# A hybrid attention and gating trunk: projections merged into the attention's stream by whole accumulations

## The chip, the core and the metric

The kernel runs on one core of a Trainium2 chip. The metric is the time of one execution on the device, in microseconds (us). A core has TensorE (PE in the rows; its weight loads are PEld), VectorE (DVE), ScalarE (ACT), GpSimd (POOL) and SyncE (SP), which here only issues transfers. Each engine works through its own list of instructions in order; engines wait for one another by semaphores.

## What is computed

Two layers with RMS norms and residuals, on 1024 tokens of width 1024, in float32. The first mixes tokens by causal attention of 16 heads (128 + 64 wide queries and keys, 128 wide values), from low-rank latents `c_q` (384) and `c_kv` (256); the second by a gated unit with a triangular 128 x 128 matrix per group. Cut to what matters:

```
h = xn @ w_in
c_q, c_kv, k_r, gate = jnp.split(h, ...)
q  = (rms_norm(c_q) @ w_uq)            # per head: 128 without, 64 with rotation
kv = (rms_norm(c_kv) @ w_ukv)          # per head: key 128, value 128
s  = (q_nope @ k_nope + q_rope @ k_rope) * ATTN_SCALE
p  = softmax(where(causal, s, neg))
o  = (p @ v) * silu(gate)
x  = x + o @ w_o
x  = x + sgu_branch(rms_norm(x)) ; y = rms_norm(x)
```

## The kernel before

Every product is made of three matmuls: an operand is split into a rounded high half and a rest (`split`, L99 to L101: ACT copies the high half, DVE or POOL subtracts it), and `mm3` (L119 to L123) adds high times high, high times rest and rest times high in one PSUM bank.

Heads are worked through in pairs, n = 0 to 15, in `attention`. A head has ten steps. In a step PE transposes blocks of the probabilities (`transpose`, tile `pt`, one bank), ACT and DVE split them into `th` and `tl`, and one step later PE multiplies them with the values (`product`, tile `pv`). Between these stand the scores of the same head's later query tiles (4 to 7) and of the next head's first ones (0 to 3): `score(n, i)` writes a score tile `s` (two banks), adds the mask on DVE (L596), takes the maximum (L598), scales it (L599), and lets ACT take the exponential with its sum (L601); DVE inverts the sum and scales the probabilities `p0` to `p7` (L602, L603). The score of tile i is up to 1024 wide; from tile 4 on it has two parts of three products each, and two matmuls for the rotated half behind each (L588, L589).

What fills the stream is the projection work: keys (`key`) and queries (`query`) of the next head by `proj_items` (L427), values of a later pair by `val` (L513), and the output projection of the pair before by `out_proj` (L529), whose block of 512 columns is added to the residual `xt` by DVE (L543). These accumulate in the two banks of the pool `ps_g` (tiles `pj`, `pv`, `po`). Each returns a list of items (cost, function): before, a projection gives one item of cost 650 for each of its nk products, a value tile four items of 330, an output projection sixteen items of 650.

What sets the order: `merge` (L440) takes two lists and puts an item of the second behind the first item of the first list at which the second's share of cost, up to the item's middle, is no greater than the first's. For each step the main items (transposes, products, scores) are merged with as many filling items as the table `target` (L695) asks for. `cut` (L681) counts how many of the output projection's items stand ahead of the key and query of the second half. Then a scheduler orders instructions by readiness, so a list is not quite the order of the engines.

The last output projection (second half of the last pair) is returned as `self.rest` and merged in `sgu` (L939) with the normalization of the first half: `share_first` spreads the inverse norms by PE (tile `rb`, L187), `quarter` normalizes (L912) and splits (L101) the operands `x1`, `x2` of the first products (`pb`, `py`, `px`, L811). `x3` is another such operand.

Of the kernel before, what the change touches and what calls it, by code (L numbers as in the profile page):

```python
# [23 lines left out]
KT = D // P  # L24
# [42 lines left out]
class Builder:  # L67
# [359 lines left out]
    def proj_items(self, w, xs, nk, h, ps, evac):  # L427
        st = {}
        c = slice(h * HALF, (h + 1) * HALF)

        def go(k):
            if k == 0:
                st["b"] = ps.tile([P, HALF], F32, tag="g", name=self.nm("pj"))
            wh, wl = w()
            self.mm3(st["b"], wh[:, k], wl[:, k], xs[0][:, k, c], xs[1][:, k, c], k == 0, k == nk - 1)
            if k == nk - 1:
                evac(st["b"])
        return [(650, lambda k=k: go(k)) for k in range(nk)]

    @staticmethod  # L440
    def merge(a, b):
# [11 lines left out]
    def attention(self, st, cq, ckv, ka, kb):  # L453
# [24 lines left out]
        def load_val(p):  # L478
            WV[p] = self.weights(a["w_kv"][p], [P, 2, 256])

        def load_out(p):
            WO[p] = [self.weights(a["w_o"][2 * p + j], [P, D]) for j in range(2)]
# [30 lines left out]
        def val(p, t2):  # L513
            st = {}

            def go(i, k):
                if (i, k) == (0, 0):
                    st["b"] = ps.tile([P, HALF], F32, tag="g", name=self.nm("pv"))
                tok = slice((2 * t2 + i) * P, (2 * t2 + i + 1) * P)
                self.mm3(  # L520
                    st["b"][:, i * 256:(i + 1) * 256], ckv[0][:, k, tok], ckv[1][:, k, tok],
                    WV[p][0][:, k], WV[p][1][:, k], k == 0, k == 1,
                )
                if (i, k) == (1, 1):
                    V[p, t2] = tile_("vh", bufs=6), tile_("vl", bufs=6)
                    self.split(*V[p, t2], st["b"])
            return [(330, lambda i=i, k=k: go(i, k)) for i in range(2) for k in range(2)]

        def out_proj(p, h):  # L529

            st = {}

            def go(m, j):
                if j == 0:
                    pool, tag = self.banks[m % len(self.banks)]
                    st[m] = pool.tile([P, HALF], F32, tag=tag, name=self.nm("po"))
                oh, ol = O[p, j, h]
                wh, wl = WO[p][j]
                c = slice(m * P, (m + 1) * P)
                self.mm3(st[m], wh[:, c], wl[:, c], oh, ol, j == 0, j == 1)  # L540
                if j == 1:
                    x = self.x[m][:, half(h)]
                    nc.vector.tensor_tensor(x, x, st[m], op=ALU.add)  # L543
                    if p == NPAIR - 1 and h == 0:
                        square(m)
                    elif p == NPAIR - 1:
                        self.residual(m)
            return [(650, lambda m=m, j=j: go(m, j)) for m in range(KT) for j in range(2)]

        def first_sums():  # L550
            b = ps.tile([P, HALF], F32, tag="g", name=self.nm("ssq"))[:, :4]
# [121 lines left out]
        for n in range(NH):  # L673
            p, j = n // 2, n % 2
            nxt = n + 1 if n + 1 < NH else None
            sc = sum((score(n, i) for i in range(4, NT)), [])
            slots = [sc[:8], sc[8:12], sc[12:13], sc[13:], []]
            sn = [score(nxt, i) for i in range(4)] if nxt is not None else [[]] * 4
            slots += [[], sn[0] + sn[1], sn[2] + sn[3], [], []]
            fill = []  # L680
            cut = 8 + j  # L681
            if j == 0:
                fill += val(p, 2) + val(p, 3) if p else []
                wo = out_proj(p - 1, 1) if p else []
            else:
                wo = [(0, lambda: load_out(p))] + out_proj(p, 0)
            if nxt is not None:
                fill += [(0, lambda: load_head(nxt))] + key(nxt, 0) + query(nxt, 0) if n else []
                if j == 1:
                    fill += [(0, lambda: load_val(p + 1))] + val(p + 1, 0) + val(p + 1, 1)  # L690
                fill += wo[:cut] + key(nxt, 1) + query(nxt, 1) + wo[cut:]
            else:
                fill += wo
            steps = apply(n)
            target = [800, 1600, 1550, 1500, 2500, 2800, 2400, 1600, 2000, 1350]  # L695
            if nxt is None:
                target[:5] = [0] * 5
            scale = sum(c for c, _ in fill) / sum(target)
            used = cum = fi = 0
            tail = []  # L700
            if nxt is None:
                fill, tail = fill[:-8], fill[-8:]
            for s in range(10):
                main = [steps[s][0]] + pending + slots[s]
                pending = [steps[s][1]]
                cum += target[s] * scale
                f0 = fi
                while fi < len(fill) and (used < cum or s == 9):
                    used += fill[fi][0]
                    fi += 1  # L710
                emit(self.merge(main, fill[f0:fi]))
# [629 lines left out]
```

## Time and profile before

| | us |
|---|---|
| median of three runs | 1711.21 |
| lowest, highest | 1710.19, 1712.98 |
| the profiled execution | 1713.96 |
| its span in the profile | 1712.2 |
| TensorE busy | 1664.5 (97%) |
| VectorE busy | 1083.9 (63%) |
| ScalarE busy | 724.5 (42%) |
| GpSimd busy | 566.9 (33%) |

The span is the time from the first to the last instruction of the profiled execution; the execution's own time has 1.76 us more around it. Stages are read by windows of the span: up to about 321 us the first projections and gates; from about 321 to 984 the attention; then the second mixer. A window row gives each engine's busy time in it with the number of its instructions, and the clock that TensorE was granted (1.00 is 2.4 GHz). An engine busy in all of a window waits for nothing there.

### The profile page before, as it was taken

What the parts mean: (1) busy time and instruction counts of PE and PEld (TensorE: products, weight loads), DVE (VectorE), ACT (ScalarE), POOL (GpSimd) and SP (SyncE); (2) the same over time, 40 slices, a digit from 0 to 9 for tenths busy, and PEclk for the clock granted to TensorE, in tenths of its full rate; (3) what the DMA queues carried; (4) which work ended last, traced back from release to release, by engine and by line L of the source; (5) the groups of instructions that cost most, each with busy time, mean ns of one, the idle gap of its engine ahead of it and who ended that gap; (6) DMA issues with size and microseconds to landing.
All of it is one profiled execution on the core that took longest, in us unless ns stands there. A gap on an engine that the chain in (4) does not pass through costs nothing. (4 is left out here: it accounts for less than half of the span.)

```text
span 1712.2 us, 23934 instructions
## 1 busy us (share of the span) xinstructions
PE 1664.5 (97%) x9142; PEld 1442.3 (84%) x9142; DVE 1083.9 (63%) x1983; ACT 724.5 (42%) x1285; POOL 566.9 (33%) x423
## 2 busy tenths in 40 slices
PE   8899999999999999999999988999999999899997
PEld 7788888888888888888888867889999888688886
DVE  7352111687777777777777699545555444688967
ACT  6222221554545454444444456433333335544234
POOL 4435561211212121212121323232112242676663
PEclk9899999999999999999999999999999999999998
DMA  6234552211101011101010333223332144633202
GB/s 191 59 94 142 166 171 88 80 41 31 53 32 53 32 53 32 53 32 53 32 57 20 107 116 112 75 91 111 107 110 99 50 160 141 209 111 148 105 25 99
DMA packets 69539, 151.55 MB, mean 89 GB/s; under 512 B 11440, under 2 KB 21168, under 8 KB 68400
## 3 DMA queue, kind: packets, MB, share of 16 engines
q1 hardware_dynamic: 59808, 126.95, 22.9%
q10 hardware_dynamic: 9616, 23.07, 3.7%
q8 instruction: 72, 1.18, 0.3%
q14 instruction: 43, 0.35, 0.1%
HBM read 107.12 MB, written 38.15 MB: 85 GB/s over the span
## 5 line engine op out<-in xcount | busy, mean ns | idle before, releaser
L101 POOL TENSOR_TENSOR wl<-wf,wh 128x512 fp32r<-128x512 f32 (+1 forms) x156 | 194.4, 1264 | 404.9 <-ACT wh L100 404.7
L101 POOL TENSOR_TENSOR wl<-raw,wh 128x1024 fp32r<-128x1024 f32 x36 | 87.5, 2431 | 244.0 <-ACT wh L100 213.5
L601 ACT ACTIVATE p<-s,mx 128x128 f32<-128x128 f32 (+7 forms) x128 | 95.0, 742 | 124.5 <-DVE mx L599 122.7
L100 ACT ACTIVATE th<-pt 128x512 fp32r<-128x512 f32 (+1 forms) x160 | 88.4, 552 | 139.2 <-PE pt L625 138.5
L100 ACT ACTIVATE wh<-wf 128x512 fp32r<-128x512 f32 (+2 forms) x158 | 86.9, 581 | 101.5 <-PE pj L122 70.2
L121 PE MATMUL pj<-xnh,wh 128*128 128x512 f32 x304 | 120.5, 396 | 0.0
L811 PE MATMUL px<-x,wh 128*128 128x512 f32 x384 | 118.8, 391 | 1.6 <-ACT x L100 1.5
L122 PE MATMUL pj<-xnl,wh 128*128 128x512 f32 x304 | 120.1, 395 | 0.0
L123 PE MATMUL pj<-xnh,wl 128*128 128x512 f32 x304 | 119.9, 395 | 0.0
L101 DVE TENSOR_TENSOR tl<-pt,th 128x512 fp32r<-128x512 f32 (+1 forms) x160 | 101.1, 632 | 27.4 <-ACT th L100 26.4
L121 PE MATMUL po<-x,wh 128*128 128x512 f32 (+1 forms) x288 | 110.8, 385 | 0.0
L122 PE MATMUL po<-x,wh 128*128 128x512 f32 (+1 forms) x288 | 106.7, 370 | 1.4 <-POOL x L101 1.4
L543 DVE TENSOR_TENSOR xt<-xt,po 128x512 f32<-128x512 f32 x128 | 87.5, 683 | 32.3 <-PE po L123 31.5
L123 PE MATMUL po<-x,wl 128*128 128x512 f32 (+1 forms) x288 | 106.9, 371 | 0.0
L121 PE MATMUL po<-oh,wh 128*128 128x512 f32 x256 | 106.0, 414 | 0.0
L123 PE MATMUL po<-oh,wl 128*128 128x512 f32 x256 | 100.8, 394 | 0.0
L122 PE MATMUL po<-ol,wh 128*128 128x512 f32 x256 | 100.6, 393 | 0.0
L598 DVE TENSOR_REDUCE mx<-s 128x1 f32<-128x128 f32 (+7 forms) x128 | 96.9, 757 | 2.9
L1122 DVE TENSOR_TENSOR xt<-xt,po 128x512 f32<-128x512 f32 (+1 forms) x144 | 86.4, 621 | 16.7 <-PE po L123 15.1
L625 PE MATMUL pt<-ident,p 128*128 128x128 f32 x576 | 90.3, 273 | 0.5 <-DVE p L603 0.4
L811 PE MATMUL py<-x,wh 128*128 128x512 f32 x256 | 82.6, 402 | 6.3 <-DVE x L101 5.0
L811 PEld LDWEIGHTS px<-x,wh 128*128 128x128 f32 x384 | 71.8, 188 | 17.1 <-ACT x L100 1.9
(268 smaller groups left out, 4799.6 us busy)
## 6 DMA issues: line engine op xcount, KB each, us to landing
raw<-w_u_dram SPq DMA_DIRECT2D x18, 512.0 KB, 3.5
raw<-w_sg_dram SPq DMA_DIRECT2D x18, 512.0 KB, 3.6
wf<-w_gate_dram SPq DMA_DIRECT2D x32, 256.0 KB, 4.2
gate<-gate ACTq DMA_DIRECT2D x16, 512.0 KB, 3.7
wf<-w_o_dram SPq DMA_DIRECT2D x32, 256.0 KB, 2.8
gate<-gate SPq DMA_DIRECT2D x32, 256.0 KB, 2.7
raw<-w_v_dram SPq DMA_DIRECT2D x16, 512.0 KB, 3.4
v<-xt ACTq DMA_DIRECT2D x32, 256.0 KB, 2.0
```

Of the source, the lines that this page charges most:

```text
L100: self.nc.scalar.activation(hi, src, AF.Copy)
L101: (eng or self.nc.vector).tensor_tensor(lo, src, hi.bitcast(F32), op=ALU.subtract)
L121: nc.tensor.matmul(out, lh, rh, start=first, stop=False)
L122: nc.tensor.matmul(out, lh, rl, start=False, stop=False)
L123: nc.tensor.matmul(out, ll, rh, start=False, stop=last)
L543: nc.vector.tensor_tensor(x, x, st[m], op=ALU.add)
L598: nc.vector.tensor_reduce(mx, b, axis=AX.X, op=ALU.max)
L601: nc.scalar.activation(pr, b, AF.Exp, bias=mx, scale=SCALE, accum_out=sm)
L625: nc.tensor.transpose(b[:, w:w + P], PR[n, 4 * h + i][:, k * P:(k + 1) * P], self.ident)
L811: nc.tensor.matmul(o, l_, m_, start=opens and n == k == e == 0, stop=closes and n == 2 and k == 3 and e == (kind == "v"), skip_group_check ...
L1122: nc.vector.tensor_tensor(x, x, b, op=ALU.add)
```

## The change

Filling items become whole accumulations: a key or query projection is one item of cost 650 x nk, a value tile one of 1320, an output block (two heads) one of 1300. The numbers that count items are halved to match: `cut` is 4 + j, and the last head keeps four items back in place of eight. Since each function still issues the same instructions in the same order within an item, what changes is where the items stand.

```
--- before.py
+++ after.py
@@ -435,7 +435,7 @@
             self.mm3(st["b"], wh[:, k], wl[:, k], xs[0][:, k, c], xs[1][:, k, c], k == 0, k == nk - 1)
             if k == nk - 1:
                 evac(st["b"])
-        return [(650, lambda k=k: go(k)) for k in range(nk)]
+        return [(650 * nk, lambda: [go(k) for k in range(nk)])]
 
     @staticmethod
     def merge(a, b):
@@ -524,7 +524,7 @@
                 if (i, k) == (1, 1):
                     V[p, t2] = tile_("vh", bufs=6), tile_("vl", bufs=6)
                     self.split(*V[p, t2], st["b"])
-            return [(330, lambda i=i, k=k: go(i, k)) for i in range(2) for k in range(2)]
+            return [(1320, lambda: [go(i, k) for i in range(2) for k in range(2)])]
 
         def out_proj(p, h):
 
@@ -545,7 +545,7 @@
                         square(m)
                     elif p == NPAIR - 1:
                         self.residual(m)
-            return [(650, lambda m=m, j=j: go(m, j)) for m in range(KT) for j in range(2)]
+            return [(1300, lambda m=m: [go(m, j) for j in range(2)]) for m in range(KT)]
 
         def first_sums():
             b = ps.tile([P, HALF], F32, tag="g", name=self.nm("ssq"))[:, :4]
@@ -678,7 +678,7 @@
             sn = [score(nxt, i) for i in range(4)] if nxt is not None else [[]] * 4
             slots += [[], sn[0] + sn[1], sn[2] + sn[3], [], []]
             fill = []
-            cut = 8 + j
+            cut = 4 + j
             if j == 0:
                 fill += val(p, 2) + val(p, 3) if p else []
                 wo = out_proj(p - 1, 1) if p else []
@@ -699,7 +699,7 @@
             used = cum = fi = 0
             tail = []
             if nxt is None:
-                fill, tail = fill[:-8], fill[-8:]
+                fill, tail = fill[:-4], fill[-4:]
             for s in range(10):
                 main = [steps[s][0]] + pending + slots[s]
                 pending = [steps[s][1]]
```

The scheduler turns this into the following at three places. Names carry running numbers that differ between the two; an arrow points from operands to result.

VectorE at the end of a head's tile 4 score (640 wide, tile `p4`) and the start of the next (`p5`), in an even head; `vl` is the low half of a value tile. Before:

```order
L596 TENSOR_TENSOR s_1161_6152<-s_1161_6152,cmask_80 128x128
L598 TENSOR_REDUCE mx_1162_6167<-s_1161_6152 128x1
L599 TENSOR_SCALAR mx_1162_6167<-mx_1162_6167 128x1
L596 TENSOR_TENSOR s_1165_6175<-s_1165_6175,cmask_80 128x128
L602 RECIPROCAL sm_1163_6168<-sm_1163_6168 128x1
L598 TENSOR_REDUCE mx_1166_6190<-s_1165_6175 128x1
L603 TENSOR_SCALAR p4_1164_6171<-p4_1164_6171,sm_1163_6168 128x640
L599 TENSOR_SCALAR mx_1166_6190<-mx_1166_6190 128x1
L101 TENSOR_TENSOR tl_1171_6203<-pt_1169_6198,th_1170_6202 128x384
```

After:

```order
L596 TENSOR_TENSOR s_1160_6148<-s_1160_6148,cmask_80 128x128
L101 TENSOR_TENSOR vl_1163_6171<-pv_1161_6157,vh_1162_6170 128x512
L598 TENSOR_REDUCE mx_1164_6177<-s_1160_6148 128x1
L596 TENSOR_TENSOR s_1167_6185<-s_1167_6185,cmask_80 128x128
L599 TENSOR_SCALAR mx_1164_6177<-mx_1164_6177 128x1
L598 TENSOR_REDUCE mx_1168_6197<-s_1167_6185 128x1
L101 TENSOR_TENSOR tl_1173_6210<-pt_1171_6205,th_1172_6209 128x384
L602 RECIPROCAL sm_1165_6178<-sm_1165_6178 128x1
L599 TENSOR_SCALAR mx_1168_6197<-mx_1168_6197 128x1
L603 TENSOR_SCALAR p4_1166_6181<-p4_1166_6181,sm_1165_6178 128x640
```

The value's split `vl` now stands between mask (L596) and maximum (L598), and the next tile's mask ahead of the scaling of the maximum (L599).

ScalarE at the same place; `oh` is the split of the head's output, `th` the high half of transposes, `vh` that of a value. Before:

```order
L100 ACTIVATE th_1156_6133<-pt_1155_6128 128x512
L100 ACTIVATE oh_1158_6144<-gate_1108_5897 128x512
L601 ACTIVATE p4_1164_6171,sm_1163_6168<-s_1161_6152,mx_1162_6167 128x640
L100 ACTIVATE th_1170_6202<-pt_1169_6198 128x384
L100 ACTIVATE vh_1172_6209<-pv_1160_6148 128x512
L601 ACTIVATE p5_1168_6194,sm_1167_6191<-s_1165_6175,mx_1166_6190 128x768
```

After:

```order
L100 ACTIVATE th_1156_6133<-pt_1155_6128 128x512
L100 ACTIVATE oh_1158_6144<-gate_1108_5897 128x512
L100 ACTIVATE vh_1162_6170<-pv_1161_6157 128x512
L100 ACTIVATE th_1172_6209<-pt_1171_6205 128x384
L601 ACTIVATE p4_1166_6181,sm_1165_6178<-s_1160_6148,mx_1164_6177 128x640
L601 ACTIVATE p5_1170_6201,sm_1169_6198<-s_1167_6185,mx_1168_6197 128x768
```

A value's `vh` and the transposes' `th` now stand ahead of the exponential of `p4`; before, both stood behind it.

TensorE at the same place; `pv` with `ckv` is a value projection, `s` is the score. Before:

```order
L123 MATMUL s_1161_6152<-k1h_1119_5959,ql_1130_6008 128x256
L121 MATMUL pv_1160_6148<-wh_1077_5779,ckv0_115 128x256
L122 MATMUL pv_1160_6148<-wl_1078_5780,ckv0_115 128x256
L123 MATMUL pv_1160_6148<-wh_1077_5779,ckv1_116 128x256
L588 MATMUL s_1161_6152<-ka_119,qs_1122_5973 128x256
L589 MATMUL s_1161_6152<-kb_120,qs_1122_5973 128x256
L121 MATMUL s_1165_6175<-k0h_1055_5693,qh_1129_6007 128x512
L122 MATMUL s_1165_6175<-k0l_1056_5694,qh_1129_6007 128x512
```

After:

```order
L121 MATMUL pv_1161_6157<-wh_1076_5774,ckv0_115 128x256
L122 MATMUL pv_1161_6157<-wl_1077_5775,ckv0_115 128x256
L123 MATMUL pv_1161_6157<-wh_1076_5774,ckv1_116 128x256
L121 MATMUL pv_1161_6157<-wh_1076_5774,ckv0_115 128x256
L122 MATMUL pv_1161_6157<-wl_1077_5775,ckv0_115 128x256
L123 MATMUL pv_1161_6157<-wh_1076_5774,ckv1_116 128x256
L588 MATMUL s_1160_6148<-ka_119,qs_1122_5967 128x256
L589 MATMUL s_1160_6148<-kb_120,qs_1122_5967 128x256
L121 MATMUL s_1167_6185<-k0h_1051_5678,qh_1125_5992 128x512
```

The value's twelve matmuls (the last six are shown) stand in one run ahead of the score's last two (L588, L589); before, six of the twelve stood ahead of them (three are shown), and the other six behind.

VectorE at the next head's first two scores (`p0`, `p1`); `ql` is the low half of a query projection. Before:

```order
L596 TENSOR_TENSOR s_1224_6438<-s_1224_6438,cmask_80 128x128
L598 TENSOR_REDUCE mx_1225_6445<-s_1224_6438 128x1
L599 TENSOR_SCALAR mx_1225_6445<-mx_1225_6445 128x1
L602 RECIPROCAL sm_1226_6446<-sm_1226_6446 128x1
L603 TENSOR_SCALAR p0_1227_6449<-p0_1227_6449,sm_1226_6446 128x128
L596 TENSOR_TENSOR s_1228_6456<-s_1228_6456,cmask_80 128x128
L598 TENSOR_REDUCE mx_1231_6470<-s_1228_6456 128x1
L101 TENSOR_TENSOR ql_1230_6464<-pj_1223_6434,qh_1229_6463 128x512
L599 TENSOR_SCALAR mx_1231_6470<-mx_1231_6470 128x1
L101 TENSOR_TENSOR tl_1236_6484<-pt_1234_6478,th_1235_6483 128x512
L602 RECIPROCAL sm_1232_6471<-sm_1232_6471 128x1
L603 TENSOR_SCALAR p1_1233_6474<-p1_1233_6474,sm_1232_6471 128x256
```

After:

```order
L596 TENSOR_TENSOR s_1223_6434<-s_1223_6434,cmask_80 128x128
L598 TENSOR_REDUCE mx_1227_6455<-s_1223_6434 128x1
L101 TENSOR_TENSOR ql_1226_6449<-pj_1224_6438,qh_1225_6448 128x512
L599 TENSOR_SCALAR mx_1227_6455<-mx_1227_6455 128x1
L596 TENSOR_TENSOR s_1230_6463<-s_1230_6463,cmask_80 128x128
L101 TENSOR_TENSOR tl_1236_6484<-pt_1234_6478,th_1235_6483 128x512
L602 RECIPROCAL sm_1228_6456<-sm_1228_6456 128x1
L598 TENSOR_REDUCE mx_1231_6470<-s_1230_6463 128x1
L603 TENSOR_SCALAR p0_1229_6459<-p0_1229_6459,sm_1228_6456 128x128
L599 TENSOR_SCALAR mx_1231_6470<-mx_1231_6470 128x1
L543 TENSOR_TENSOR xt_66<-xt_66,po_1237_6493 128x512
L602 RECIPROCAL sm_1232_6471<-sm_1232_6471 128x1
L603 TENSOR_SCALAR p1_1233_6474<-p1_1233_6474,sm_1232_6471 128x256
```

The two softmaxes now lie within each other, with `ql` and `tl` between.

VectorE where the second mixer begins; L912 normalizes, L101 splits, L543 adds an output block. Before:

```order
L912 SCALAR_TENSOR_TENSOR xt_66<-xt_66,ng_67,rb_1997_9886 128x512 x3
L101 TENSOR_TENSOR x1_1980_9851<-xt_66,x1_1980_9851 128x512 x3
L543 TENSOR_TENSOR xt_66<-xt_66,po_2009_9967 128x512
L912 SCALAR_TENSOR_TENSOR xt_66<-xt_66,ng_67,rb_1997_9886 128x512 x2
L543 TENSOR_TENSOR xt_66<-xt_66,po_2010_9983 128x512
L101 TENSOR_TENSOR x1_1980_9851<-xt_66,x1_1980_9851 128x512
L101 TENSOR_TENSOR x2_1984_9855<-xt_66,x2_1984_9855 128x512
L912 SCALAR_TENSOR_TENSOR xt_66<-xt_66,ng_67,rb_1997_9886 128x512 x2
L543 TENSOR_TENSOR xt_66<-xt_66,po_2011_9999 128x512
```

After:

```order
L912 SCALAR_TENSOR_TENSOR xt_66<-xt_66,ng_67,rb_1997_9886 128x512 x2
L543 TENSOR_TENSOR xt_66<-xt_66,po_2009_9967 128x512
L101 TENSOR_TENSOR x1_1980_9851<-xt_66,x1_1980_9851 128x512 x2
L912 SCALAR_TENSOR_TENSOR xt_66<-xt_66,ng_67,rb_1997_9886 128x512 x2
L543 TENSOR_TENSOR xt_66<-xt_66,po_2010_9983 128x512
L101 TENSOR_TENSOR x1_1980_9851<-xt_66,x1_1980_9851 128x512 x2
L912 SCALAR_TENSOR_TENSOR xt_66<-xt_66,ng_67,rb_1997_9886 128x512 x2
L543 TENSOR_TENSOR xt_66<-xt_66,po_2011_9999 128x512
```

The additions now stand after every two normalizing steps and every two splits.

## Rows read from the trace of the kernel before

**Rows 1.** Windows of the span: busy us (instructions) of PE, PEld, DVE, ACT, POOL; clock; DMA share, GB/s

```profile
300.00:352.00 52.00, 49.07 (x293) 41.58 (x292) 38.34 (x92) 29.56 (x61) 10.86 (x12) 1.00 0.24 78
...
380.00:940.00 560.00, 560.00 (x3323) 494.96 (x3322) 417.65 (x902) 259.79 (x535) 108.43 (x112) 1.00 0.13 41
...
984.00:1082.00 98.00, 87.46 (x373) 69.32 (x372) 92.67 (x119) 58.49 (x82) 27.55 (x14) 0.98 0.33 111
```

**Rows 2.** Waits, 952 to 1080 us: total us, times, longest us

```profile
PE py L811 <- DVE x L101: 5.0, 3, 2.3
```

**Rows 3.** Timeline, tile 4's score: start, us, engine, line, operation, tiles [idle before]

```profile
648.44 0.28 PE L588 MATMUL s<-ka,qs 128*128 128x256 f32 x1
...
648.56 0.28 PE L589 MATMUL s<-kb,qs 128*128 128x256 f32 x1
...
648.88 0.30 DVE L596 TENSOR_TENSOR s<-s,cmask 128x128 f32<-128x128 f32 x1 [0.95 <-PE s L589]
...
649.21 0.82 DVE L598 TENSOR_REDUCE mx<-s 128x1 f32<-128x640 f32 x1
...
650.32 0.79 ACT L601 ACTIVATE p<-s,mx 128x640 f32<-128x640 f32 x1 [1.73 <-DVE mx L599]
651.01 0.19 ACT L601 ACTIVATION_READ_ACCUMULATOR p<-s,mx 128x1 f32 x1
651.38 0.49 ACT L100 ACTIVATE th<-pt 128x384 fp32r<-128x384 f32 x1 [0.17 <-PE pt L625]
...
652.53 0.40 PE L121 MATMUL s<-k0h,qh 128*128 128x512 f32 x1
652.76 0.40 PE L122 MATMUL s<-k0l,qh 128*128 128x512 f32 x1
```

**Rows 4.** Timeline of VectorE, a value's split and what follows it

```profile
911.49 0.68 DVE L101 TENSOR_TENSOR vl<-pv,vh 128x512 fp32r<-128x512 f32 x1
912.09 0.14 DVE L599 TENSOR_SCALAR mx<-mx 128x1 f32<-128x1 f32 x1
```

**Rows 5.** Timeline, the next head's first scores

```profile
674.73 0.27 PE L589 MATMUL s<-kb,qs 128*128 128x128 f32 x1
...
676.75 0.28 PE L589 MATMUL s<-kb,qs 128*128 128x256 f32 x1
...
678.97 0.19 ACT L601 ACTIVATION_READ_ACCUMULATOR p<-s,mx 128x1 f32 x1
...
680.29 0.40 PE L121 MATMUL s<-k0h,qh 128*128 128x512 f32 x1
```

**Rows 6.** Timeline, the second half of an even head

```profile
685.20 0.69 DVE L504 TENSOR_TENSOR qs<-gate,qs 64x512 fp32r<-64x512 f32 x1
...
685.92 0.49 DVE L603 TENSOR_SCALAR p<-p,sm 128x512 f32<-128x512 f32 x1
...
687.10 3.00 POOL L101 TENSOR_TENSOR wl<-wf,wh 128x512 fp32r<-128x512 f32 x2 [8.44 <-ACT wh L100]
...
687.50 1.44 DVE L504 TENSOR_TENSOR qs<-gate,qs 64x512 fp32r<-64x512 f32 x1
```

**Rows 7.** Timeline at the second mixer's start; the last row is from the chain of waits

```profile
1012.63 0.50 PE L187 MATMUL rb<-work,ones_r 128*128 128x512 f32 x1
...
1014.80 0.39 PE L811 MATMUL pb<-x,wl 128*128 128x512 f32 x1
...
1065.06 2.36 POOL L101 TENSOR_TENSOR wl<-raw,wh 128x1024 fp32r<-128x1024 f32 x1 [3.93 <-ACT wh L100]
1065.22 5.03 DVE L101 TENSOR_TENSOR x<-xt,x 128x512 fp32r<-128x512 f32 x3
...
1068.02 0.50 PE L811 MATMUL py<-x,wh 128*128 128x512 f32 x1 [2.29 <-DVE x L101]
...
1069.70 0.79 PE L811 MATMUL py<-x,wh 128*128 128x512 f32 x1 [0.72 <-DVE x L101]
...
1069.70 10.94 PE py L811 x41
```

More of the change, by code (lines that the diff above doesn't have):

```diff
@@ L437, in go @@
                 evac(st["b"])
-        return [(650, lambda k=k: go(k)) for k in range(nk)]
+        return [(650 * nk, lambda: [go(k) for k in range(nk)])]
     @staticmethod
@@ L526, in go @@
                     self.split(*V[p, t2], st["b"])
-            return [(330, lambda i=i, k=k: go(i, k)) for i in range(2) for k in range(2)]
+            return [(1320, lambda: [go(i, k) for i in range(2) for k in range(2)])]
         def out_proj(p, h):
@@ L547, in go @@
                         self.residual(m)
-            return [(650, lambda m=m, j=j: go(m, j)) for m in range(KT) for j in range(2)]
+            return [(1300, lambda m=m: [go(m, j) for j in range(2)]) for m in range(KT)]
         def first_sums():
@@ L680, in attention @@
             fill = []
-            cut = 8 + j
+            cut = 4 + j
             if j == 0:
@@ L701, in attention @@
             if nxt is None:
-                fill, tail = fill[:-8], fill[-8:]
+                fill, tail = fill[:-4], fill[-4:]
             for s in range(10):
```

## The prediction

> **What bounds the kernel now.** I read the windows by stage first, then the waits inside the stages that the change touches, then single chains. TensorE (PE) is busy 97% of the span (the table): what can move the time is PE's own work, or a wait that PE makes. The windows [rows 1] say where waits are: in 380 to 940 us PE is busy 560.00 of 560 us, with the granted clock at 1.00. There is no wait in it that the change could remove. Its start (300 to 352) lacks 2.9 us, and the stage behind the attention, 984 to 1082, lacks 10.5 us, with VectorE (DVE) busy 92.67 of 98: there PE waits for DVE, and the list of waits names it [rows 2]. So inside the attention the change can only lose: a reorder matters there only if it makes an operand late that was in time. The question of each step below is how much spare time the operand had.
>
> **PE's own work.** The products are the same 9,142 matmuls, of the same shapes. A 512-column one follows the next after 0.23 us, a 256-column one after 0.117 (652.53 to 652.76 and 648.44 to 648.56 [rows 3]). A switch between one accumulation and another shows no price of its own: the runs of different tiles keep these distances. The first ordinary matmul after a run of transposes stands about 0.08 late; the program has 171 such runs after, 166 before, so 5 x 0.08 = +0.4 at most; taken +0.2.
>
> **Place A, score tile 4 of each head (640 wide).** Before [rows 3]: the last matmul of the score at 648.56, the mask (L596) 648.88, the maximum (L598) 649.21, ScalarE's (ACT's) exponential (L601) at 650.32, its sum read from 651.01 to 651.20; PE needs the score bank again at 652.53. Spare: 652.53 - 651.20 = 1.33 us. Three things now come into this chain, all seen in the order:
> - The value projection's twelve matmuls stand as one block ahead of the score's last two; before, six of them did. 6 x 0.117 = +0.70, so the score ends at 649.26, the mask starts at 649.58.
> - On DVE the value's low half (`vl`) now stands between mask and maximum. One costs 912.09 - 911.49 = 0.60 [rows 4]; it waits for ACT's `vh`, which itself starts 0.3 after the last value matmul and takes 0.6, so `vl` is no earlier than about 649.98. The maximum starts about 650.58 in place of 649.21, and the next tile's mask now stands ahead of the scaling of the maximum (L599): its result comes at about 651.8.
> - On ACT the transposes' high half `th` now stands ahead of the exponential. Before it ran at 651.38 [rows 3]; its transposes come three value matmuls later, 3 x 0.117 = 0.35, so it runs at 651.73, and takes 0.49, the next following 0.10 before its end (as 651.01 follows 650.32 + 0.79 [rows 3]). The exponential starts at 652.12, in place of 650.32.
>
> By the distance of before (650.32 to 651.20, 0.88, and 0.05 for the signal) the bank is free at 653.05. PE comes to it at 652.53 + 0.35 = 652.88. Wait: about 0.17 us; for odd heads, where a key's split takes the value's place, about 0.19. Thirteen heads repeat this pattern (heads 2 to 14): 13 x 0.18 = **+2.3 us**. Bounds: the steps' error is about 0.2 us each way, so 0 to 13 x 0.4 = +5.
>
> **Place B, the first two tiles of the next head.** Before [rows 5]: score 0 ends at 674.73, score 1 at 676.75, exponential 1's sum is read until 678.97 + 0.19 = 679.16, and PE needs the bank at 680.29: spare 1.1. After, the query's nine matmuls stand in a block ahead of score 0's end, three did before: 6 x 0.23 = +1.39, 676.12, so that two softmaxes come 0.65 apart, with `ql` and `tl` between on DVE, and on ACT `th` ahead of exponential 0. Following the same distances, the bank comes free at 680.31 to 680.43. PE's place is unchanged, 680.29: 0.02 to 0.14. I take 0.05 x 13 = **+0.7**, from 0 to +1.8.
>
> **Place C, a scaling against POOL.** At the end of each even head DVE's scaling of the next head's 512-wide tile 3 (L603) runs at 685.92, and the second query split (L504) stands behind it at 687.50 [rows 6]. After, the scaling stands behind that split and another `tl`. DVE's work on SBUF alone is held while GpSimd (POOL) runs: the same split took 0.69 without and 1.44 beside POOL's 3.00 us of weight splits [rows 6]. By my working the scaling now runs from 687.56 to 688.05, POOL starts 0.1 later at about 687.67, and the fourth transpose needs it at 688.16. If the scaling gets in first, 0. If POOL does: between 0.75 (the split's own loss) and 1.5 (one POOL split), say 1.2, in each of 7 heads, 8.4. In the sum it is 0; the margin of 0.1 us makes it a rival. The Trainium skill, page "GPSIMD Engine Reference", section "1. Specifications", says that the two engines share SBUF interfaces and contend where DVE works in its two-port mode or with two SBUF inputs; the rows of the split agree. By that the scaling, of one input, would be held only in that mode; and the sum is the same by either.
>
> **Bank order.** Output blocks of both halves use two banks, and a block now closes before the next opens; the third waits for the addition (L543) of the first, with 0.4 to 0.8 us to spare. Price 0, up to +0.4 in a few heads; the cover is the six matmuls of the second block (6 x 0.23 = 1.4 us). Also the loads on SP's queue and POOL's splits are reached by the same counts of work: 0.
>
> **Start of the attention (300 to 352).** 2.9 us of waits [rows 1]; the items move, no wait there is touched directly: 0, from -1 to +1.
>
> **Entry of the next mixer (984 to 1082).** The last eight output blocks are merged with the normalization's steps; eight items of 1300 in place of sixteen of 650 put DVE's additions earlier among the normalizing steps. Two things can come of it. The second spreading matmul (`rb`, L187) of the second half stands behind all of one `pb` accumulation in place of its middle: before it began at 1012.63, the block's last matmul at 1014.80 [rows 7], so it comes at 1015.03 at the earliest, 2.4 us later, and DVE's next work (L912) waits for it: +2.4, up to +2.9. Against it, the same rows show DVE held by POOL: three `x` splits that took 5.03 us beside POOL's 2.36, for which PE waited 2.29 and 0.72 us, and whose wait was followed by a clock at half: 41 matmuls took 10.94 us, at 0.23 each 9.43, so 1.5 lost. If the two pass each other, 2.29 + 0.72 + 1.5 = 4.5 come back. I give that two chances in five: 2.4 - 0.4 x 4.5 = **+0.6**, between -4.5 and +2.9.
>
> **Sum.** 0.2 + 2.3 + 0.7 + 0 + 0 + 0 + 0.6 = +3.8 us. Against the profiled execution, 1713.96: 1717.8. That execution is 2.75 us above the median of the runs, 1711.21; the difference is what I trust, so 1711.21 + 3.8 = **1715.0 us**.
>
> **Rivals.**
> - *Nothing to measure.* Places A and B turn out to have their 0.2 us of spare after all (each chain ends within 0.2 us of PE's need), the entry evens out: 0 to +3 us, 1711 to 1714. For it: PE is busy 100% now, and both waits are smaller than the error of their working. Against: both places err on the same side, and thirteen times.
> - *Faster.* The entry gives back its 4.5, `rb` costs nothing since what stands behind it is late anyway, and A and B stay at zero: 1711.2 - 4.5 + 0.2 = about 1707. For it: the DVE rows there are stretched by chance of timing. Against: the new place of `rb`.
> - *Slower by much.* Place C: POOL gets in 0.1 us before DVE; it decides from there, and costs 7 x 1.2 = 8.4: 1715.0 + 8.4 = 1723.4. For it: the margin is below the error. Against: POOL's start follows ACT's weight split, which itself is not earlier than before.
> - *The clock.* Many small waits could make the clock fall, as one of 0.72 did at 1069.70 [rows 7]. At 1.5 us a fall and 26 waits this is +39: 1754 with the rest. Against it: the start, 300 to 352, has 2.9 us of waits in it and keeps 1.00 [rows 1]. The Trainium skill, "TensorE: Matmul & The Clock Gate", section "A second HAM failure mode: psum-queue depth-cycling", describes a kernel whose clock swings since PE idles briefly between groups of matmuls while it goes round its banks. By that rule the two places would cost far more than their waits; the row of 300 to 352 speaks against it here.
> - *The change does not do what it says*: excluded by the order, where 179 of 204 accumulations of the stage stand unbroken, 59 did.
>
> **How the numbers follow.** A change under 0.2% (3.4 us) is about what the measurement of this kernel can't tell from none. My case, +3.8 with A at 0.18, has chance 0.40; its sum lies so near 3.4 that 0.27 of this is above and 0.13 below. Place C has 0.15, nothing to measure 0.29, faster 0.11, the clock 0.02, and losses of a like size that I have not found 0.03. Together: faster 0.11, same 0.29 + 0.13 = 0.42, slower 0.27 + 0.15 + 0.02 + 0.03 = 0.47. The range leaves out the faster rival, the clock and the top of place C (0.05), 0.18 in all: 1711.0 to 1724.0.
>
> **What would show it.** After: 380 to 940 is no longer 560.00; PE waits for ACT's exponential (`s` from `p`, L121 of the score tiles) in two places of each head, 0.1 to 0.3 us each. At the 640-wide tile, ACT's order is `th`, then exponential. If place C holds, DVE's L603 on 128x512 takes over 1 us and PE's transposes (L625) wait for it. The clock stays at 1.00 through the stage; at the entry, waits for `x` (L101) shrink or grow from the 5.0 us [rows 2]. A wrong forecast would show as no PE wait in the attention and the whole difference between 984 and 1082, or as PE matmuls closer than 0.23 and 0.117 us apart.

## The result

The changed kernel takes 1724.71 us (median of six runs, 1723.21 to 1725.88) against 1710.76 us of six runs before: 1.0078 of it, with a 95% interval of 1.0068 to 1.0088, that is 14 us slower. The forecast was 1715.0, from 1711.0 to 1724.0. The direction was right, the size was not: the cost is nearly four times the forecast +3.8.

Windows of the changed kernel, against [rows 1] (busy us of PE, PEld, DVE, ACT, POOL, clock, DMA share, GB/s):

```profile
300.00:352.00 52.00, 50.04 (x301) 42.87 (x302) 40.10 (x96) 29.97 (x63) 9.27 (x11) 1.00 0.21 67
...
380.00:940.00 560.00, 554.52 (x3249) 481.80 (x3248) 401.53 (x872) 249.98 (x516) 104.92 (x108) 1.00 0.13 41
...
984.00:1082.00 98.00, 86.52 (x365) 68.18 (x364) 87.12 (x123) 56.25 (x81) 31.38 (x16) 0.96 0.37 127
```

From 380 to 940 us PE now lacks 5.5 us of busy time, and 74 of 3323 matmuls are missing from the window: they come later. What PE waits for between 300 and 1090 us in the changed kernel, against [rows 2] (total us, times, longest):

```profile
PE pt L625 <- DVE p L603: 5.0, 6, 0.8
PE py L811 <- ACT x L100: 4.1, 1, 4.1
PE py L811 <- DVE x L101: 2.5, 2, 1.8
PE pb L811 <- DVE xt L543: 2.4, 1, 2.4
```

The first row is place C: the fourth transpose of six heads waits for DVE's scaling. It was a rival with chance 0.15, and it came true.

I laid the two traces over each other by TensorE's work: for each matmul of before, when the changed kernel has done as much. Between 380 and 940 us of before the changed kernel falls behind by 12.5 us, in steps that repeat with each pair of heads; from 300 to 380 by 0.4, from 940 to 984 by 0.0. So 12.9 us are lost inside the attention. (The two spans differ by only 9.5 us, since the executions that were profiled differ elsewhere: from 20 to 60 us, long before anything that was changed, the granted clock was 0.91 in the one of before and 1.00 in the other, and the one of before is 3 us above its median.) A distance between two matmuls that is more than 0.13 us over the usual one counts as a wait here; with the usual distances as in the prediction, and 0.11 between transposes, the 12.5 us are:

| place | waits, us | first matmul after each, us | together |
|---|---|---|---|
| C, fourth transpose (L625) | 6, 5.95 | | 5.95 |
| A, the score that takes tile 4's bank (L121 of `s`) | 13, 2.37 | 13 x 0.107 | 3.8 |
| an output block's bank (L121 of `po`) | 6, 1.25 | 6 x 0.107 | 1.9 |
| the rest: six delays of 0.11 before the first transpose at place C, and many of some hundredths | | | 0.9 |

**Place C in the changed kernel** (timeline of DVE, ACT, POOL and PE; start, duration, engine), against [rows 6]:

```profile
689.15 0.14 DVE L599 TENSOR_SCALAR mx<-mx 128x1 f32<-128x1 f32 x1
...
690.38 1.67 ACT L100 ACTIVATE wh<-wf 128x512 fp32r<-128x512 f32 x3
...
690.72 0.54 DVE L101 TENSOR_TENSOR tl<-pt,th 128x384 fp32r<-128x384 f32 x1
...
691.09 2.69 POOL L101 TENSOR_TENSOR wl<-wf,wh 128x512 fp32r<-128x512 f32 x2 [9.59 <-ACT wh L100]
...
691.17 1.47 DVE L603 TENSOR_SCALAR p<-p,sm 128x512 f32<-128x512 f32 x1
...
691.32 0.55 PE L625 MATMUL pt<-ident,p 128*128 128x128 f32 x3
692.69 0.33 PE L625 MATMUL pt<-ident,p 128*128 128x128 f32 x1 [0.83 <-DVE p L603]
```

POOL began 0.08 us before the scaling, which took 1.47 us where it took 0.49 before. The transpose that reads it started 1.10 us after the third one in place of 0.11. The three transposes ahead of it are late as well, by 0.11 us: they start 0.05 us after `tl`, which frees the transposes' one bank, ends at 691.26.

Both rivals of this race start at one instruction, DVE's scaling of the maximum (L599, 689.15). On DVE the scaling comes 2.02 us behind it. On ACT the exponential waits for it, then come `th` and the first copy of the weights (690.38), and POOL's split follows that copy, 1.93 us behind L599. All six heads show the same two numbers.

**Place A in the changed kernel**, against [rows 3]:

```profile
652.37 0.28 PE L589 MATMUL s<-kb,qs 128*128 128x256 f32 x1
...
652.69 0.30 DVE L596 TENSOR_TENSOR s<-s,cmask 128x128 f32<-128x128 f32 x1 [1.61 <-PE s L589]
653.08 0.69 DVE L101 TENSOR_TENSOR vl<-pv,vh 128x512 fp32r<-128x512 f32 x1
653.69 0.81 DVE L598 TENSOR_REDUCE mx<-s 128x1 f32<-128x640 f32 x1
...
654.83 0.49 ACT L100 ACTIVATE th<-pt 128x384 fp32r<-128x384 f32 x1 [1.79 <-PE pt L625]
655.22 0.79 ACT L601 ACTIVATE p<-s,mx 128x640 f32<-128x640 f32 x1
...
655.85 0.28 PE L123 MATMUL pv<-wh,ckv 128*128 128x256 f32 x1
655.89 0.20 ACT L601 ACTIVATION_READ_ACCUMULATOR p<-s,mx 128x1 f32 x1
656.15 0.50 PE L121 MATMUL s<-k0h,qh 128*128 128x512 f32 x1
656.48 0.39 PE L122 MATMUL s<-k0l,qh 128*128 128x512 f32 x1
```

The chain is the one forecast, `vl` ahead of the maximum and `th` ahead of the exponential. PE's matmul comes 0.30 after the one before, in place of 0.117: a wait of 0.18. No bracket marks it as idle, because the record of the matmul before runs until 656.13. And the matmul behind it follows after 0.33 in place of 0.23.

**Place B in the changed kernel**, against [rows 5]: the sum of exponential 1 is read in time, and the score that follows starts without a gap.

```profile
683.31 0.20 ACT L601 ACTIVATION_READ_ACCUMULATOR p<-s,mx 128x1 f32 x1
...
683.54 0.34 PE L589 MATMUL s<-kb,qs 128*128 128x384 f32 x1
683.72 0.40 PE L121 MATMUL s<-k0h,qh 128*128 128x512 f32 x1
```

**An output block's bank in the changed kernel** (timeline of DVE and PE, an odd head): the addition that frees the bank stands behind the maximum of the 1024-wide score.

```profile
712.39 1.23 DVE L598 TENSOR_REDUCE mx<-s 128x1 f32<-128x1024 f32 x1
713.53 0.68 DVE L101 TENSOR_TENSOR tl<-pt,th 128x512 fp32r<-128x512 f32 x1
...
714.19 0.68 DVE L543 TENSOR_TENSOR xt<-xt,po 128x512 f32<-128x512 f32 x1
...
714.92 0.50 PE L121 MATMUL po<-oh,wh 128*128 128x512 f32 x1
```

The block that is added had its last matmul at 712.28; the addition comes at 714.19, and PE's next block starts 0.05 us after it ends. Its second matmul stands 0.65 us behind the transpose ahead of the block, where a block behind transposes had 0.34 in the kernel before: 0.31 late, six times.

### The profile page after: what moved, and what is told of

The parts are those of the page before. It is cut to its first block, busy times and chain, and to the rows that moved or that the text cites. A ratio compares the mean times of both kernels' runs of the same rounds, so it can differ in the third digit from the quotient of the medians.

```text
span 1721.7 us, 23937 instructions
## 1 busy us (share of the span) xinstructions
PE 1667.8 (97%) x9142; PEld 1435.7 (83%) x9142; DVE 1075.9 (62%) x1983; ACT 721.2 (42%) x1285; POOL 567.4 (33%) x423
## 5 line engine op out<-in xcount | busy, mean ns | idle before, releaser
L101 POOL TENSOR_TENSOR wl<-wf,wh 128x512 fp32r<-128x512 f32 (+1 forms) x156 | 192.7, 1253 | 366.3 <-ACT wh L100 366.0
L101 POOL TENSOR_TENSOR wl<-raw,wh 128x1024 fp32r<-128x1024 f32 x36 | 87.7, 2437 | 244.1 <-ACT wh L100 208.8
L121 PE MATMUL pj<-xnh,wh 128*128 128x512 f32 x304 | 119.2, 392 | 0.0
L121 PE MATMUL po<-x,wh 128*128 128x512 f32 (+1 forms) x288 | 110.0, 382 | 0.6 <-ACT x L100 0.6
L101 DVE TENSOR_TENSOR tl<-pt,th 128x512 fp32r<-128x512 f32 (+1 forms) x160 | 100.9, 631 | 12.4 <-ACT th L100 12.2
L101 POOL TENSOR_TENSOR ol<-gate,oh 128x512 fp32r<-128x512 f32 x30 | 38.7, 1292 | 207.8 <-ACT oh L100 207.8
L121 PE MATMUL po<-oh,wh 128*128 128x512 f32 x256 | 104.1, 407 | 0.3
L543 DVE TENSOR_TENSOR xt<-xt,po 128x512 f32<-128x512 f32 x128 | 87.5, 683 | 18.1 <-PE po L123 15.9
L598 DVE TENSOR_REDUCE mx<-s 128x1 f32<-128x128 f32 (+7 forms) x128 | 96.4, 754 | 2.6
L625 PE MATMUL pt<-ident,p 128*128 128x128 f32 x576 | 92.8, 274 | 5.1 <-DVE p L603 5.0
L625 PEld LDWEIGHTS pt<-ident,p 128*128 128x128 f32 x576 | 70.5, 140 | 25.6 <-DVE p L603 6.9
```

The lines of the kernel that those rows point to most:

```text
L101: (eng or self.nc.vector).tensor_tensor(lo, src, hi.bitcast(F32), op=ALU.subtract)
L121: nc.tensor.matmul(out, lh, rh, start=first, stop=False)
L598: nc.vector.tensor_reduce(mx, b, axis=AX.X, op=ALU.max)
L625: nc.tensor.transpose(b[:, w:w + P], PR[n, 4 * h + i][:, k * P:(k + 1) * P], self.ident)
```

## Experiments

The times of a kernel below stand against runs of the kernel before on the same chip (medians 1712.6 to 1713.7 us there). Where it says "in the attention", it is the loss from 380 to 940 us against the trace of before, laid over by TensorE's work as above (12.5 for the changed kernel).

### Each part alone

```
-        return [(650, lambda k=k: go(k)) for k in range(nk)]        # p_only: this line alone
+        return [(650 * nk, lambda: [go(k) for k in range(nk)])]
-            return [(330, ...) for i in range(2) for k in range(2)]   # v_only: this line alone
+            return [(1320, lambda: [go(i, k) for i in range(2) for k in range(2)])]
-            return [(650, ...) for m in range(KT) for j in range(2)]  # o_only: this, cut = 4 + j, fill[:-4]
+            return [(1300, lambda m=m: [go(m, j) for j in range(2)]) for m in range(KT)]
```

*v_only.* 

> The kernel before with the value projection alone made whole (one item of 1320). Theory of places: place A of the seven even heads (score tile 4) waits, since the value's twelve matmuls, its split and the transposes' high half come into that chain: a wait of 0.18 us and a first matmul 0.11 late, 0.30 x 7 = +2.1 us; nothing in odd heads, nothing at place C, 0 at the entry. Rival, a price of unbroken accumulations on TensorE itself, spread over all 204: 28 of them, 13 x 28/204 = +1.8 us, with no wait at one place but each matmul of the run a little late. The two are told apart by the distances of matmuls: one of 0.42 us at tile 4 of each even head, or many of a little over 0.117.

Measured: 1.0006 (0.9997 to 1.0015); in the attention +2.2 us, in seven places. The place in one even head (timeline of PE):

```profile
654.00 0.28 PE L123 MATMUL pv<-wh,ckv 128*128 128x256 f32 x1
654.28 0.50 PE L121 MATMUL s<-k0h,qh 128*128 128x512 f32 x1
654.61 0.40 PE L122 MATMUL s<-k0l,qh 128*128 128x512 f32 x1
```

Seven waits of 0.16, each with the 0.10 behind it. So the value's block makes place A of the even heads, and its unbroken accumulations show no price of their own. In this kernel's window from 380 to 940 us PE is "busy" 559.99 of 560, while 2.2 us are lost.

*p_only.* 

> The kernel before with key and query projections alone made whole. Theory of places: place A of the odd heads waits (the key's split k0h and th stand ahead of the exponential on ScalarE): 0.31 x 6 = +1.9 us; place B stays without a wait; at place C the scaling does not stand behind the second query split, so TensorE does not wait there; entry unchanged. Rival, a price of unbroken accumulations: 58 of 204, 13 x 58/204 = +3.7 us.

Measured: 1.0032 (1.0019 to 1.0045); in the attention +5.4. Six waits at place A of the odd heads, as expected, but of 0.48 us, not 0.19, and six of 0.14 for an output block's bank. The waits were at the named place and their size was not right; a_swap, below, shows what adds to them.

*o_only.* 

> The kernel before with output blocks alone made whole (the last projection too), and the two counts halved. Theory of places: place C, the scaling of the 512-wide tile behind the second query split and held by GpSimd: 1.1 x 6 = +6.6 us; third output block waiting for its bank in odd heads, 0.32 x 6 = +1.9; the entry of the next mixer +2.2: +10.7 us in all, and no wait at place A. Rival, a price of unbroken accumulations: 118 of 204, 13 x 118/204 = +7.5 us and the entry's 2.2, without a wait at place C.

Measured: 1.0003 (0.9994 to 1.0012); in the attention +2.0, without a wait of the fourth transpose at place C. A miss, and the one that tells most. DVE's order at place C is the one of the changed kernel, and yet (timeline of ACT, DVE and POOL):

```profile
686.79 1.68 ACT L100 ACTIVATE wh<-wf 128x512 fp32r<-128x512 f32 x3 [0.21 <-PE po L122]
686.82 0.54 DVE L101 TENSOR_TENSOR tl<-pt,th 128x384 fp32r<-128x384 f32 x1
687.27 0.48 DVE L603 TENSOR_SCALAR p<-p,sm 128x512 f32<-128x512 f32 x1
...
687.51 2.65 POOL L101 TENSOR_TENSOR wl<-wf,wh 128x512 fp32r<-128x512 f32 x2 [9.29 <-ACT wh L100]
```

The scaling starts 0.24 us before POOL, takes 0.48, and is done 0.08 us before the transpose wants it. In the changed kernel POOL is 0.08 us ahead. So place C is a race, and the output blocks alone don't lose it. The scaling comes 2.02 us behind L599 as in the changed kernel; POOL comes 2.26 behind it and not 1.93, because ACT's copy waits for PE's last read of the old weights.

The output block's bank shows here by itself (timeline of DVE and PE, an odd head), with the addition behind the 1024-wide scaling:

```profile
710.49 0.68 DVE L543 TENSOR_TENSOR xt<-xt,po 128x512 f32<-128x512 f32 x1
710.82 0.49 PE L625 MATMUL pt<-ident,p 128*128 128x128 f32 x3
711.22 0.50 PE L121 MATMUL po<-oh,wh 128*128 128x512 f32 x1
```

The block starts 0.05 us after the addition ends, and its second matmul 0.53 us after the last transpose, 0.19 late: six of these are 1.1 us, where +1.9 was expected. Most of the other 0.9 us stands before transposes that wait for `tl`. The three parts alone add up to 2.2 + 5.4 + 2.0 = 9.6 us in the attention, but only to 0.41% in the times; the whole change costs 0.78%.

### The last output projection

```
+            if (p, h) == (NPAIR - 1, 1):    # r_only: whole blocks here alone; a_restfine: the reverse
```

*r_only.* 

> The kernel before with only the last output projection (the one merged with the next mixer's normalization) in whole blocks. Theory: the attention stays as it was, busy 560.00 of 560; only 984 to 1082 us changes, by +2.2 us as in the changed kernel. Rival: the entry's difference is chance of one execution: 0.

Measured: 0.9999 (0.9989 to 1.0008); the attention is unchanged (0.0). From 984 to 1095 us the trace is 2.1 us later than that of before, but the time is the same.

*a_restfine.* 

> The changed kernel with the last output projection alone in sixteen items of 650. Theory: the attention keeps its 13 us, the entry goes back to that of before: 2.2 us less than the changed kernel, 1722.5. Rival, the entry's difference is chance of one execution: 1724.7.

Measured: 1.0075 (1.0060 to 1.0090), 12.5 in the attention, and 1.4 us behind before from 984 to 1095. The undone part gives nothing back that can be measured. In v_only, which doesn't touch that stage's items, the same stretch is 1.7 us behind the trace of before; in o_only, which has that projection in whole blocks, 0.4. So the forecast's term for the entry isn't borne out: the difference there is no more than executions differ by.

### Undoing the value projection

*a_vfine.* 

> The changed kernel with the value projection undone (four items of 330). Theory of places: place A of the even heads goes back to no wait, 2.1 us less than the changed kernel: 1722.6; odd heads, place C and the entry stay. Rival (price of unbroken accumulations): 1.8 less, without a single place. If the wait at tile 4 stays in even heads, the value's block is not its cause.

Measured: 1.0053 (1.0038 to 1.0068); in the attention 9.4, 3.1 less than the changed kernel. The waits of even heads at tile 4 are gone, those of odd heads (six of 0.19) and the six of place C (5.97) stay. The delay of an output block behind its bank shrinks from 0.31 to the 0.19 us of o_only, too little for the count of waits, which was not expected. Between 380 and 945 us the only wait of PE long enough to be listed:

```profile
PE pt L625 <- DVE p L603: 5.0, 6, 0.8
```

With o_only and p_only this shows that the lost race of place C needs two parts together, key and query projections and output blocks.

### What holds the scaling at place C

*a_nopool.*

```
-            self.split(h[:, c], l[:, c], f[:, :n], eng or nc.gpsimd)
+            nc.scalar.activation(h[:, c], f[:, :n], AF.Copy) if raw else self.split(...)
-        return r(h), r(l)
+        return r(h), r(h if raw else l)          # raw: output weights of pairs 1 to 6
```

> The changed kernel without GpSimd's low half of the output projection's weights (pairs 1 to 6): ACT still makes the high half, and the matmuls read it in place of the low half, so GpSimd has nothing to do at place C; VectorE's order there is the same. This part of the computation is changed. Theory (VectorE's scaling is held while GpSimd runs): the 512-wide scaling takes 0.5 to 0.6 us in place of 1.47, the fourth transpose waits 0 to 0.1 in place of 0.83, 6 x 1.0 = 6 us less than the changed kernel, 1718.5. Rival (the scaling is late by its place in VectorE's order alone): the wait stays at 0.8 us, 1724.5.

Measured: 1721.15 us, 1.0046 (1.0029 to 1.0062). Same order on DVE, no POOL there (timeline of DVE):

```profile
691.03 0.54 DVE L101 TENSOR_TENSOR tl<-pt,th 128x384 fp32r<-128x384 f32 x1
691.48 0.48 DVE L603 TENSOR_SCALAR p<-p,sm 128x512 f32<-128x512 f32 x1
```

0.48 us, and the transpose doesn't wait. So POOL's work is what stretches the scaling, not the scaling's place. But in the attention only 3.8 us came back (8.7 in place of 12.5) where 6.0 were expected: the waits at place A grew from 2.4 to 4.4 us in total.

*a_p3act.*

```
-                nc.vector.tensor_scalar(pr, pr, sm, None, op0=ALU.mult)
+                nc.scalar.activation(pr, pr, AF.Copy, scale=sm) if (i, n % 2) == (3, 1) else nc.vector.tensor_scalar(...)
```

> The changed kernel with the scaling of the 512-wide tile 3 of odd heads on ScalarE in place of VectorE. By the order it stands there behind the transposes' high half and one weight copy, so from about 691.0 to 691.6 where VectorE's ran 691.17 to 692.64. Theory (held on VectorE by GpSimd, ScalarE is not held): the fourth transpose waits 0 to 0.15 us in place of 0.83, 5 to 6 us less than the changed kernel: 1718.7 to 1719.7. Rival (any engine that works on SBUF alone is held by GpSimd): the scaling takes over 1.2 us on ScalarE too, the wait stays at 0.8: 1724.5.

Measured: 1.0050 (1.0034 to 1.0066); in the attention 7.4, 5.1 less, and no wait of the fourth transpose. ACT's scaling takes 0.72 us (timeline of ACT and POOL):

```profile
689.06 0.72 ACT L603 ACTIVATE p<-p,sm 128x512 f32<-128x512 f32 x1
...
689.25 3.79 POOL L101 TENSOR_TENSOR wl<-wf,wh 128x512 fp32r<-128x512 f32 x3 [9.59 <-ACT wh L100]
...
689.68 0.63 ACT L100 ACTIVATE wh<-wf 128x512 fp32r<-128x512 f32 x1
```

The scaling starts 0.19 us ahead of POOL, and one that starts ahead isn't held on DVE either (o_only). So this run doesn't tell the theory from its rival by the scaling. The copy behind it does, SBUF to SBUF as well: it starts with a split of POOL in hand and takes 0.63 us. Between 300 and 990 us of this run twenty 512-wide copies start so and take 0.62 to 0.63; thirty beside an idle POOL take 0.62 to 0.64. So ACT's copies are not held where DVE's scaling was.

*a_step256.*

```
-            WO[p] = [self.weights(a["w_o"][2 * p + j], [P, D]) for j in range(2)]
+            WO[p] = [self.weights(a["w_o"][2 * p + j], [P, D], step=256 if p else HALF) for j in range(2)]
```

> The changed kernel with the output weights of pairs 1 to 7 copied and split in pieces of 256 columns in place of 512, so that one piece keeps GpSimd busy about 0.65 us in place of 1.27. Theory (VectorE's scaling is held to the end of the piece that GpSimd has begun): the transpose's delay at place C falls from 0.99 to 0.3 to 0.5 us, 3 to 4 us less than the changed kernel in the attention. Rival (the scaling runs at a lower speed all the while GpSimd works, whatever the size of a piece): 0.99 stays.

Measured: 1.0054 (1.0038 to 1.0070); in the attention 9.1, 3.4 less. The transpose's delay fell from 0.99 to 0.25 (six together 1.49). Timeline of POOL and DVE:

```profile
691.21 2.31 POOL L101 TENSOR_TENSOR wl<-wf,wh 128x256 fp32r<-128x256 f32 x3 [9.41 <-ACT wh L100]
...
691.51 0.71 DVE L603 TENSOR_SCALAR p<-p,sm 128x512 f32<-128x512 f32 x1
```

The scaling starts 0.30 us into POOL's work and takes 0.71, not 1.47, although POOL goes on for 2 us. The first piece takes POOL 0.74 us; the scaling ends 0.28 us after the piece that POOL had in hand when it started, as it does beside the 512-wide one. So what holds it is that piece, not POOL's working as such.

*a_swap.*

```
-                self.mm3(st[m], wh[:, c], wl[:, c], oh, ol, j == 0, j == 1)
+                for q, (l_, r_) in enumerate(((wh, oh), (wl, oh), (wh, ol))): nc.tensor.matmul(st[m], l_[:, c], r_, ...)
```

> The changed kernel with the three matmuls of each output product in the order high by high, rest of the weights by high, high by rest (the last two change places), so that a weights' high half is read once more behind the transposes, 1.1 us later than in the changed kernel. Theory (at place C a race: GpSimd's weight split starts 0.08 us before VectorE's scaling, and the split's start hangs on the buffer that TensorE's last read frees): ScalarE's weight copy starts about 0.3 us later, GpSimd's split too, VectorE's scaling is first, takes 0.5 us, and the fourth transpose no longer waits: 6.0 us less than the changed kernel, about 1718.5. Rival (the scaling is late by its place alone, or is held whichever starts first): the wait of 0.83 us stays, 1724.5.

Measured: 1724.92 us (four runs, 1720.27 to 1725.28), 1.0067 (1.0049 to 1.0085). Place C comes out as the theory has it (timeline of ACT, DVE and POOL): the scaling is first, by 0.24 us, and the transpose doesn't wait.

```profile
692.17 1.67 ACT L100 ACTIVATE wh<-wf 128x512 fp32r<-128x512 f32 x3 [0.21 <-PE po L540]
...
692.64 0.48 DVE L603 TENSOR_SCALAR p<-p,sm 128x512 f32<-128x512 f32 x1
...
692.88 2.64 POOL L101 TENSOR_TENSOR wl<-wf,wh 128x512 fp32r<-128x512 f32 x2 [9.95 <-ACT wh L100]
```

In the changed kernel TensorE's last read of the old weights' high half (689.09) is long over when ACT comes to the copy, right behind `th`: what the theory says of POOL's start doesn't hold there. Here the last read stands behind the transposes, at 691.74, ACT's copy waits 0.21 us for it, and POOL comes 2.26 us behind L599 in place of 1.93. So the race can be turned by the time of that read. The time is a miss, though: in the attention 9.3 in place of 12.5, 3.2 us came back of 6.0, and even those the four runs don't show beyond their spread. The rest went to place A of the odd heads, which now wait 0.6 us and not 0.19. ACT there, first in the changed kernel:

```profile
695.61 0.62 ACT L100 ACTIVATE wh<-wf 128x512 fp32r<-128x512 f32 x1
696.34 0.60 ACT L100 ACTIVATE k0h<-pj 128x512 fp32r<-128x512 f32 x1
...
699.10 0.79 ACT L601 ACTIVATE p<-s,mx 128x640 f32<-128x640 f32 x1
```

and in a_swap:

```profile
697.13 0.63 ACT L100 ACTIVATE wh<-wf 128x512 fp32r<-128x512 f32 x1 [0.81 <-DMA wf<-w_o_dram]
697.66 0.58 ACT L100 ACTIVATE k0h<-pj 128x512 fp32r<-128x512 f32 x1
...
700.00 0.80 ACT L601 ACTIVATE p<-s,mx 128x640 f32<-128x640 f32 x1 [0.31 <-DVE mx L599]
```

The last piece of the weights comes from memory too late, its copy waits 0.81 us for it at the head of ACT's queue, and behind it stand the key's split, on it DVE's `k0l`, then the maximum, then the exponential. While PE stood still at place C, the load had that time for nothing. The load needs one of three buffers (`wf`), and the traces show it issued where POOL's first split ends and frees one: at 692.38 against 692.36 in the changed kernel, at 694.30 against 694.27 here. No run has more buffers, so what that would give isn't shown.

*a_swap_vhalf.*

```
-            return [(1320, lambda: [go(i, k) for i in range(2) for k in range(2)])]
+            return [(660, lambda i=i: [go(i, k) for k in range(2)]) for i in range(2)]    # and a_swap's edit
```

> The changed kernel with the order of the output products of the run before and the value projection in two items of 660 in place of one of 1320. Theory of places: place C gone (-6.0), and at tile 4 of even heads the value's split no longer stands ahead of the exponential with the transposes' high half behind it, so that place A waits in odd heads alone (-2.0): 8 us less than the changed kernel, about 1716.5. If the value's whole block is not the cause at tile 4, even heads wait 0.18 us as before: 1718.5.

Measured: 1716.79 us, 1.0024 (1.0014 to 1.0034); in the attention 5.2. The fourth transpose and the even heads wait no more, nor do output blocks; six waits of 0.6 us in odd heads are most of what is left (3.7, with 0.6 behind them). The time is as expected, in part by luck: the odd heads wait longer than the theory had it, and the bank's waits, which it left in, are gone. It doesn't beat the kernel before, which had no wait here to lose.

## Why the prediction fell short

- **What bounds the kernel** held: PE was full in the attention, the change could only lose there, and there it lost 12.9 of 14 us.
- **TensorE's own work.** The +0.2 us for runs of transposes isn't there. The matmul behind a run takes 0.31 us to its successor and not 0.23, but it follows the last transpose after 0.03 us and not 0.11: the two cancel.
- **Place A** was right in place, order and wait: 13 waits of 0.18 us, forecast 0.18. The sum had 2.3 us and the trace has 3.8: the step that failed is that a wait costs its own length. The matmul behind it starts 0.33 us after, not 0.23, 13 x 0.107 = 1.4 us more.
- **Place B** was forecast at +0.7; 0 of it came. The sum is read until 683.51 and PE starts at 683.72.
- **Place C** is the step that broke the sum. Its working had the scaling at 687.56 and POOL at 687.67, a lead of 0.1 us for the scaling, and put the likelier side, 0, into the sum. Laid over by TensorE's work, POOL starts where it was forecast, at 687.68 of before's time, but the scaling only at 687.74, 0.18 later than worked out, so POOL had the lead. So the step that failed is DVE's chain up to the scaling; which of its instructions was placed too early can't be told, since the prediction gives only the end of that working. The reason it gave against the rival, that ACT's weight split "itself is not earlier than before", held (the copy and POOL come 0.6 later than before) and decided nothing, since the scaling moved by 1.8. The price of the rival, 1.2 us in 7 heads, was near (0.99 in 6). A margin of 0.1 us, below the error of the steps that gave it, stood at 0.15 of a chance; with half of its 8.4 in the sum the forecast would have been 1719.2.
- **Bank order** was priced at 0, up to +0.4 us; six delays cost 1.9. The cover that was named, the six matmuls of the second block, is shorter than the 1.9 us for which the addition stands behind the maximum and a split. Whole output blocks alone cost 1.1 of it (o_only); with the value's block added it is 1.9 (the changed kernel against a_vfine).
- **Entry**, +0.6 by a loss of 2.4 and a chance of 4.5: the runs show no effect beyond what executions differ by (r_only, a_restfine).
- **The clock** stayed at 1.00 from 380 to 940 through 25 waits of 0.2 to 1.0 us. The rival that follows the Trainium skill ("TensorE: Matmul & The Clock Gate", "A second HAM failure mode: psum-queue depth-cycling") is not borne out here. The fall that it took as its example came behind two waits, of 2.29 and 0.72 us [rows 7], not behind one of 0.72.
- **Contention.** The Trainium skill ("GPSIMD Engine Reference", "1. Specifications") names DVE's two-port mode or two SBUF inputs as the cases of contention. The scaling reads one tile and a column of scalars, and was held: 1.47 us against 0.48 without POOL. The trace agrees with the page if this form works in that mode, which no run here shows by itself. What the rows of before show is its speed: 0.35, 0.49 and 0.75 us for 256, 512 and 1024 columns, 0.07 per 128, where the split `tl` takes 0.13 per 128 (0.55 for 384, 0.68 for 512).

In sum: 3.8 (A) + 5.95 (C) + 1.9 (bank) + 0.9 (the rest) + 0.4 (300 to 380) = 12.9 us, of the 14 measured (interval of the ratio: 11.6 to 15.1).

## What to carry to other kernels

Where the busiest engine has no wait left, a coarser interleave can only cost, and its price lies in the queues of the other engines: look for what now stands ahead of each operand's last step. A forecast can't call two operations with a margin of 0.1 us between them, and the outcome is the same in each turn of the loop (0.08 us in all six heads here): half of its price belongs into the sum, not into a tail. And a stall that is removed takes with it the time that it gave to others: of the 6 us of place C only 3.2 to 5.1 came back.

## What the runs showed of the hardware

- A wait of up to about 0.16 us behind a 256-column matmul doesn't show as idle time in this profile: the records last 0.28 us and follow each other every 0.117. A window that says 560.00 of 560 can hide 2 us; the distances between starts show it.
- After a wait the first 512-column matmul takes 0.10 to 0.11 us longer to its successor than in a run (0.33 against 0.23, 13 of them at place A of the changed kernel, 7 in v_only). Behind a run of transposes it takes 0.31 without a wait.
- DVE's scaling of a 128x512 tile in SBUF that starts while GpSimd has a split in hand ends 0.28 us after that split does, whether the split is 512 or 256 columns wide (1.47 and 0.71 us in place of 0.48); one that starts 0.24 us before GpSimd isn't held. The trace of before has the like: its 128-wide scaling at 342.24, started 0.09 us behind a split of POOL, takes 1.29 us in place of 0.29 and ends 0.08 after that split. ACT's copies from SBUF to SBUF are not held (0.63 us either way).

```profile
342.24 1.29 DVE L603 TENSOR_SCALAR p<-p,sm 128x128 f32<-128x128 f32 x1
```
